# A fixed order of TensorE's instructions through an attention stage, with merge products dealt out between its steps

## The chip, the core and the metric

The kernel runs on one core of a Trainium2 chip. The metric is the device time of one execution in microseconds (us), median of several runs. The engines have queues of their own and meet through semaphores: TensorE (PE; its weight loads are shown as PEld) multiplies into PSUM, VectorE (DVE) and ScalarE (ACT) work on PSUM and SBUF, GpSimd (POOL) on SBUF alone, SyncE (SP) issues most DMAs, and ACT issues a few.

## The reference

One decoder layer on 512 tokens of width 1024, in float32. The input is normalized and projected; three mixers work on the projection (sparse attention, a spatial-gating MLP, RWKV-7); each result is gated, projected to 1024 channels and merged, and an output projection, a gated embedding and a last normalization follow.

```python
proj = h @ w_in[i]
y_nsa = _nsa(...)      # attention: block-compressed, selected and window keys
y_sg = _spatial_gating(...)
y_rk = _rwkv7(...)
ys = jnp.stack([y_nsa * jax.nn.silu(nz), y_sg * jax.nn.silu(sz), y_rk * jax.nn.silu(rz)], axis=2)
zs = jnp.einsum('bsnc,ncd->bsnd', ys, w_branch[i])
merge = jax.nn.sigmoid(mg).reshape(B, S, N_BRANCHES, D)
x = x + jnp.sum(merge * zs, axis=2) @ w_o[i]
```

Attention has 8 heads in 2 groups and works on query blocks of 128 tokens. With 512 tokens all eight selection blocks are always chosen, so the kernel computes the selected and the window part as causal attention over all keys up to the query block, and the compressed part as attention over 31 blocks.

## The kernel before

Products keep float32 precision by splitting operands into a high half (float32r) and a remainder: where both operands are split, a product is three matmuls, high x high, high x low, low x high. Weights come by DMA as `wr` (SP), ACT casts the high half `wh`, and POOL (in some stages DVE) subtracts for the low half `wl` (`wload`, L67 to L80). `fm_block` (L150) makes one block of 128 output channels for all 512 tokens: 8 x 3 matmuls of 512 columns from the normalized input (`hH`, `hL`), or 4 x 3 from a mixer's output (`ysH`, `ysL`), into a PSUM tile `mm_ps` of a pool of two.

A merge of branch b (L789) runs over m = 0 to 7: a gate block (24 matmuls, tanh by ACT into `sg`), a product block (12 matmuls), and an evacuation by DVE into `macc` (b = 1) or into `sg` and then by POOL into `macc` (b = 2, 0). Six gate blocks of b = 1 were made earlier and come back from DRAM. Branch 1 is the spatial gating, 2 the RWKV mixer, 0 attention; the first two don't need attention, the third needs all of it.

Attention (L814 to L889) goes over query blocks i = 3, 2, 1, 0 (512, 384, 256, 128 keys). For each block, eight small products give the block scores `sc_c` of all heads, and DVE and ACT make the block probabilities `pcm` from them. For each group g of four heads, `pcm` is transposed (`pc_ps`), spread by DVE (`pd`), split into `ph` and `pl`, and begins the output `o_ps` (one buffer). For b = 0, 1 (selected, window) and four heads hh there are scores `s_ps` (three buffers: two matmuls with keys `kst`, one that adds the causal mask), their maximum `mx` (DVE), the exponential with its sum (ACT), a reciprocal and a product with the gate (DVE, `sm`), and a scaling of the probabilities `P` (two heads by DVE, one by ACT, one by POOL). For each key tile kt, four transpositions give `p_ps`; ACT casts the high half `ph`, DVE subtracts for the low half `pl`, and two matmuls add to `o_ps`, the one with `pl` first. At the end of a group ACT copies half of `o_ps` (`ot`) and DVE adds both halves into `nsaY`.

A scheduler with a timing model of its own puts the instructions of each engine in order; program order is only its priority. So the merge products of branches 1 and 2, which stand behind attention in the program, go wherever it finds attention's next instruction not ready. `HOLD` (L31) keeps the last four of them until four late points of attention. Then `nsaY` is multiplied by `zs`, the gate path that is loaded from DRAM into an `sg` buffer (L898 to L901), split into `ysH` and `ysL`, and branch 0 is merged. The pool `ep` (L905: `x1`, `pp`, `fg`) is opened after attention's pools are closed, and its first loads (L910, from ACT's queue) wait until attention's tiles are let go.

Of the kernel before, what the change touches and what calls it, by code (L numbers as in the profile page):

```python
# [19 lines left out]
NG = 6  # L20
# [10 lines left out]
HOLD = (-1,) * 12 + (3, 4, 5, 6)  # L31
# [14 lines left out]
def hybrid_kernel(ctx, tc, x, p, norm_g, w_in, cmp_w1, cmp_w2, cmp_pe, sg_ln_g, sg_ln_b, sg_w, sg_b,  # L46
# [14 lines left out]
    def mm(o, a, b, start, stop, **kw):  # L61
        return PE.matmul(o, a, b, start=start, stop=stop, **kw).ins  # L62
# [726 lines left out]
    def merge(b, yH, yL, first, fin, after=()):  # L789
        for m in range(8):  # L790
          with ExitStack() as es:
            if m < len(after) and after[m] is not None:
                es.enter_context(tc.issue_after(after[m]))
            sg = gp.tile([128, 512], F32, tag="sg", name="sg")
# [12 lines left out]
            fm_block(m * 128, 128, ev_b, w_branch[b], yH, yL, 4)
# [5 lines left out]
    anch = []  # L813
    for i in ATT:  # L814
        isl = slice(i * 128, (i + 1) * 128)
        W = (i + 1) * 128
        sc = aps.tile([128, 8, 64], F32, tag="pt", name="sc_c", bufs=BP)
        for h in range(8):
            mm(sc[:, h, :], qst[:, h // 2, h % 2, isl], kcst[:, h // 4].rearrange("p a n -> p (a n)"), True, True)
# [10 lines left out]
        gv = gate[:, i, :].rearrange("p (h b) -> p b h", b=3)  # L830
# [5 lines left out]
        for g in range(2):  # L836
            o_ps = aps.tile([128, 512], F32, tag="o", name="o_ps", bufs=BO)
            pc_ps = aps.tile([128, 128], F32, tag="pt", name="pc_ps", bufs=BP)
            PE.transpose(pc_ps, pcm[:, 4 * g:4 * g + 4, :].rearrange("p h n -> p (h n)"), ident)
            pd = ap_.tile([128, 4, 128], F32, tag="pd", name="pd", bufs=1)  # L840
            ph = ap_.tile([128, 512], R, tag="ph", name="ph", bufs=3)
            pl = ap_.tile([128, 512], R, tag="pl", name="pl", bufs=3)
            V.tensor_tensor(pd, pc_ps.unsqueeze(1).to_broadcast([128, 4, 128]),
                            hm.unsqueeze(2).to_broadcast([128, 4, 128]), OP.mult)
            pd2 = pd.rearrange("p h t -> p (h t)")
            S.copy(ph, pd2)
            V.tensor_tensor(pl, pd2, f(ph), OP.subtract)
            mm(o_ps, vcst[:, g, :], ph, True, False)
            mm(o_ps[0:64], vcst[:, g, 0:64], pl, False, False)
            for b in range(2):  # L850
                P = ap_.tile([128, 4, 512], F32, tag="P", name="P")
                mx = ap_.tile([128, 4], F32, tag="mx", name="mx")
                sm = ap_.tile([128, 4], F32, tag="sm", name="sm")
                for hh in range(4):
                    h = g * 4 + hh
                    s_ps = aps.tile([128, 512], F32, tag="s", name="s_ps", bufs=BS)
                    qs = qst[:, h // 2, h % 2, isl]
                    mm(s_ps[:, :W], qs, kst[b][:, g, 0, :W], True, False)
                    mm(s_ps[:, :W], qs, kst[b][:, g, 1, :W], False, False)
                    mm(s_ps[:, i * 128:W], identb, trib, False, True)  # L860
                    V.tensor_reduce(mx[:, hh:hh + 1], s_ps[:, :W], axis=AX.X, op=OP.max, negate=True)  # L861
                    S.activation(P[:, hh, :W], s_ps[:, :W], AF.Exp, bias=mx[:, hh:hh + 1],  # L862
                                 accum_out=sm[:, hh:hh + 1])
                V.reciprocal(sm, sm)
                V.tensor_tensor(sm, sm, gv[:, 1 + b, g * 4:g * 4 + 4], OP.mult)
                for hh in range(4):
                    if PS[hh] == "S":
                        S.activation(P[:, hh, :W], P[:, hh, :W], AF.Copy, scale=sm[:, hh:hh + 1])
                    else:
                        (G if PS[hh] == "G" else V).tensor_scalar(P[:, hh, :W], P[:, hh, :W], sm[:, hh:hh + 1],  # L870
                                                                  None, op0=OP.mult)
                for kt in range(i + 1):
                    p_ps = aps.tile([128, 512], F32, tag="pt", name="p_ps", bufs=BP)
                    for hh in range(4):
                        PE.transpose(p_ps[:, hh * 128:hh * 128 + 128], P[:, hh, kt * 128:kt * 128 + 128], ident)  # L875
                    ph = ap_.tile([128, 512], R, tag="ph", name="ph", bufs=3)
                    pl = ap_.tile([128, 512], R, tag="pl", name="pl", bufs=3)
                    S.copy(ph, p_ps)  # L878
                    V.tensor_tensor(pl, p_ps, f(ph), OP.subtract)  # L879
                    mm(o_ps[0:64], vst[:, kt, b, g, 0:64], pl, False, False)  # L880
                    last = mm(o_ps, vst[:, kt, b, g, :], ph, False, b == 1 and kt == i)
            anch.append(last)
            ot = ap_.tile([64, 512], F32, tag="ot", name="ot", bufs=1)
            S.copy(ot, o_ps[64:128])
            o4 = o_ps.rearrange("p (a e t) -> p a e t", a=2, e=2)
            t4 = ot.rearrange("p (a e t) -> p a e t", a=2, e=2)
            for e in range(2):
                V.tensor_tensor(nsaY[e * 64:e * 64 + 64, 2 * g:2 * g + 2, isl], o4[0:64, :, e, :], t4[:, :, e, :],
                                OP.add)  # L889
    at_ctx.close()  # L890
    nsa_ctx.close()

    hold = [None if h < 0 else anch[h] for h in HOLD]
    merge(1, y1H, y1L, True, lambda m: None, hold[:8])
# [128 lines left out]
```

## Time and profile before

| | us |
|---|---|
| median of 3 runs (lowest to highest) | 746.05 (745.58 to 747.11) |
| the profiled execution's own time | 744.63 |
| its span, first to last instruction | 742.8 |
| TensorE busy | 714.5 (96%) |
| DVE, ACT, POOL busy | 408.6, 353.8, 287.0 |
| attention, first to last score product | 378.1 to 547.1 |

The shares are averages over stages. TensorE's busy time contains modelled ends: a matmul of 512 columns is shown 0.39 us long, while the next starts 0.23 us after it, so a wait is best read from the distance of two starts. An idle time at the end of a row names what ended it.

### The profile page before, as it was taken

What the parts mean: (1) busy time and instruction counts of PE and PEld (TensorE: products, weight loads), DVE (VectorE), ACT (ScalarE), POOL (GpSimd) and SP (SyncE); (2) the same over time, 40 slices, a digit from 0 to 9 for tenths busy, and PEclk for the clock granted to TensorE, in tenths of its full rate; (3) what the DMA queues carried; (4) which work ended last, traced back from release to release, by engine and by line L of the source; (5) the groups of instructions that cost most, each with busy time, mean ns of one, the idle gap of its engine ahead of it and who ended that gap; (6) DMA issues with size and microseconds to landing.
All of it is one profiled execution on the core that took longest, in us unless ns stands there. A gap on an engine that the chain in (4) does not pass through costs nothing.

```text
span 742.8 us, 13074 instructions
## 1 busy us (share of the span) xinstructions
PE 714.5 (96%) x4941; PEld 606.7 (82%) x4941; DVE 408.6 (55%) x776; ACT 353.8 (48%) x743; POOL 287.0 (39%) x275
## 2 busy tenths in 40 slices
PE   4999999999999999989999999989999999999995
PEld 4888788999878987779877778867877888998995
DVE  6531587758843863565676565397555223226345
ACT  6554555542363342335565554576554333227453
POOL 6444640120220263300144345333445565356563
PEclk9999999999999999999999999999999999999999
DMA  5853122125536364427433212201228334132212
GB/s 194 188 140 100 48 81 71 41 85 146 156 105 224 101 184 117 116 86 232 124 97 103 58 43 71 71 16 42 53 62 268 96 91 127 59 114 72 80 63 114
DMA packets 106689, 78.73 MB, mean 106 GB/s; under 512 B 5569, under 2 KB 97282, under 8 KB 106626
## 3 DMA queue, kind: packets, MB, share of 16 engines
q1 hardware_dynamic: 105890, 75.27, 35.5%
q10 hardware_dynamic: 736, 2.63, 0.9%
q8 instruction: 39, 0.64, 0.4%
q14 instruction: 24, 0.20, 0.1%
HBM read 67.91 MB, written 9.96 MB: 105 GB/s over the span
## 4 chain that ended last, share of the span: by engine, by line
PE 88%; DVE 4%; ACT 2%; DMA 2%; issue 1%; POOL 1%; SPq 1%; ACTq 0%; POOLq 0%; DVEq 0%
PE mm_ps L62 70%; PE s_ps L62 3%; PE o_ps L62 2%; PE g_ps L62 2%; PE p_ps L875 2%; DMA w1t<-in_cmp_w_dram 1%; PE Yp L62 1%; DVE mx L861 1%; PE u_ps L62 1%; ACT wh L78 1%; PE xt_ps L222 1%; PE r_ps L62 1%; PE mx_ps L62 1%; DVE pl L879 1%; PE bk_ps L477 1%
## 5 line engine op out<-in xcount | busy, mean ns | idle before, releaser
L79 POOL TENSOR_TENSOR wl<-wr,wh 128x512 fp32r<-128x512 f32 x144 | 192.6, 1346 | 278.9 <-ACT wh L78 257.6
L78 ACT CAST wh<-wr 128x512 fp32r<-128x512 f32 (+1 forms) x194 | 119.4, 620 | 166.5 <-PE mm_ps L62 114.9
L62 PE MATMUL mm_ps<-hH,wh 128*128 128x512 f32 (+1 forms) x440 | 174.9, 398 | 3.3 <-ACT wh L78 1.9
L62 PE MATMUL mm_ps<-hL,wh 128*128 128x512 f32 (+1 forms) x440 | 171.6, 390 | 0.0
L62 PE MATMUL mm_ps<-hH,wl 128*128 128x512 f32 (+1 forms) x440 | 171.1, 389 | 0.0
L62 PEld LDWEIGHTS mm_ps<-hH,wh 128*128 128x128 f32 x440 | 83.5, 190 | 20.7 <-ACT wh L78 2.2
L62 PEld LDWEIGHTS mm_ps<-hH,wl 128*128 128x128 f32 x440 | 83.2, 189 | 17.4 <-issue 0.2
L62 PEld LDWEIGHTS mm_ps<-hL,wh 128*128 128x128 f32 x440 | 83.6, 190 | 16.5 <-issue 0.2
L62 PE MATMUL mm_ps<-wh,hL 128*128 128x256 f32 (+1 forms) x224 | 65.0, 291 | 0.0
L62 PE MATMUL mm_ps<-wh,hH 128*128 128x256 f32 (+1 forms) x224 | 63.8, 286 | 0.0
L62 PE MATMUL mm_ps<-wl,hH 128*128 128x256 f32 (+1 forms) x224 | 63.7, 285 | 0.0
L79 DVE TENSOR_TENSOR wl<-wr,wh 128x512 fp32r<-128x512 f32 (+1 forms) x50 | 38.0, 768 | 26.8 <-ACT wh L78 26.7
L62 PEld LDWEIGHTS mm_ps<-wh,hL 128*128 128x128 f32 x224 | 42.2, 188 | 1.1 <-issue 0.5
L62 PEld LDWEIGHTS mm_ps<-wh,hH 128*128 128x128 f32 x224 | 42.1, 188 | 1.2 <-issue 0.5
L62 PEld LDWEIGHTS mm_ps<-wl,hH 128*128 128x128 f32 x224 | 42.2, 188 | 0.5
L879 DVE TENSOR_TENSOR pl<-p_ps,ph 128x512 fp32r<-128x512 f32 x40 | 27.1, 685 | 25.7 <-ACT ph L878 25.6
L62 PE MATMUL mm_ps<-ysH,wh 128*128 128x512 f32 x96 | 38.6, 402 | 0.1
L62 PE MATMUL mm_ps<-ysL,wh 128*128 128x512 f32 x96 | 38.4, 400 | 0.2 <-DVE ysL L725 0.2
L62 PE MATMUL mm_ps<-ysH,wl 128*128 128x512 f32 x96 | 38.2, 398 | 0.0
L862 ACT ACTIVATE P<-s_ps,mx 128x512 f32<-128x512 f32 (+3 forms) x64 | 33.4, 531 | 7.9 <-DVE mx L861 5.5
L62 PE MATMUL mm_ps<-wh,mH 128*128 128x256 f32 x128 | 35.9, 286 | 0.0
L62 PE MATMUL mm_ps<-wl,hT 128*128 128x256 f32 x128 | 35.8, 281 | 0.0
(337 smaller groups left out, 1434.6 us busy)
## 6 DMA issues: line engine op xcount, KB each, us to landing
wr<-in_w_in_dram SPq DMA_DIRECT2D x130, 256.0 KB
wr<-in_w_branch_dram SPq DMA_DIRECT2D x24, 256.0 KB
wr<-in_w_o_dram SPq DMA_DIRECT2D x16, 256.0 KB
wr<-in_w_ple_gate_dram SPq DMA_DIRECT2D x16, 256.0 KB
xs__129<-in_x_dram SPq DMA_DIRECT2D x4, 512.0 KB
w1t<-in_cmp_w_dram SPq DMA_DIRECT2D x4, 512.0 KB
x<-in_x_dram ACTq DMA_DIRECT2D x4, 512.0 KB
out_dram<-x SPq DMA_DIRECT2D x8, 256.0 KB
```

What stands on the lines that cost most here:

```text
L62: return PE.matmul(o, a, b, start=start, stop=stop, **kw).ins
L78: S.copy(h[:, :m], raw[:, :m])
L79: ph_["l"].tensor_tensor(l[:, :m], raw[:, :m], f(h[:, :m]), OP.subtract)
L222: PE.transpose(ps[:, k, :], xs_[:, t, (4 * a + k) * 128:(4 * a + k + 1) * 128], ident)
L477: PE.transpose(ps[:, c - c0, :], bk[:, c, 0:2].rearrange("p s t -> p (s t)"), ident)
L861: V.tensor_reduce(mx[:, hh:hh + 1], s_ps[:, :W], axis=AX.X, op=OP.max, negate=True)
L862: S.activation(P[:, hh, :W], s_ps[:, :W], AF.Exp, bias=mx[:, hh:hh + 1], accum_out=sm[:, hh:hh + 1])
L875: PE.transpose(p_ps[:, hh * 128:hh * 128 + 128], P[:, hh, kt * 128:kt * 128 + 128], ident)
L879: V.tensor_tensor(pl, p_ps, f(ph), OP.subtract)
```

## The change

TensorE's order through attention and through the merges of branches 1 and 2 is written out. The attention code is cut into acts: `cmp_` (block scores and `pcm`), `pc_` (transposition of `pcm`, P), `oc_` (first two matmuls of `o_ps`, C), `s_` (scores of one head with what follows, S0 to S3), `t_` (transposition of a key tile, T0 to T3), `o_` (its two matmuls, O0 to O3). A step is one (i, g, b), sixteen in all. In a step stand the scores S of the *next* step and the T, C, O of this one, in the order of the table `ORD`. `merge_gen` yields once ahead of every merge matmul, and `deal(n)` lets n of them go: 16 after the first scores (15 matmuls, since the first call only opens the block), 8 behind the first `pc_`, and 25 in each step, evenly spread over its acts. All of these matmuls are kept in program order (`keep_in_program_order`); the other engines are still ordered by the scheduler. A block's weights are asked for when the block ahead of it begins. `HOLD` goes. The loads of `nz` go into slices of `pp` instead of `sg` buffers.

```diff
-HOLD = (-1,) * 12 + (3, 4, 5, 6)
+FILL = (16, 8, 25)
...
+    def blk_gen(ws, srcH, srcL, nk, evac, ahead):
+
+        hs, ls = ws
+        ahead()
+        ps = pmm.tile([128, 512], F32, tag="mm", name="mm_ps")
+        for k in range(nk):
+            for j, (w, s) in enumerate(((hs, srcH), (hs, srcL), (ls, srcH))):
+                yield
+                pin(PE.matmul(ps, w[k], s[:, k, :], start=k == 0 and j == 0, stop=k == nk - 1 and j == 2))
+        evac(ps)
...
+    def o_(i, g, b, kt):
+        o_ps = ops[i, g]
+        ph, pl = trp.pop(kt)
+        mmp(o_ps[0:64], vst[:, kt, b, g, 0:64], pl, False, False)
+        mmp(o_ps, vst[:, kt, b, g, :], ph, False, b == 1 and kt == i)
...
+    ORD = {3: "S0 T0 C S1 T1 S2 O0 T2 S3 O1 T3 O2 P O3", 2: "S0 T0 C S1 T1 S2 O0 S3 T2 O1 P O2",
+           1: "S0 T0 C S1 S2 T1 S3 O0 P O1", 0: "S0 T0 C S1 S2 S3 P O0"}
+    fill = merge_gen(((1, y1H, y1L, True), (2, y2H, y2L, False)))
+
+    def deal(n):
+        for _ in range(n):
+            next(fill, None)
+
+    steps = [(i, g, b) for i in ATT for g in range(2) for b in range(2)]
+    cmp_(3)
+    for hh in range(4):
+        s_(*steps[0], hh)
+    deal(FILL[0])
+    pc_(3, 0)
+    deal(FILL[1])
+    for n, (i, g, b) in enumerate(steps):
+        nx = steps[n + 1] if n + 1 < len(steps) else None
+        acts = []
+        if (g, b) == (1, 0) and i > 0:
+            acts.append(lambda i=i: cmp_(i - 1))
...
+        tot = FILL[2]
+        for j, act in enumerate(acts):
+            act()
+            deal((j + 1) * tot // len(acts) - j * tot // len(acts))
+    for _ in fill:
+        pass
     at_ctx.close()
     nsa_ctx.close()
 
-    hold = [None if h < 0 else anch[h] for h in HOLD]
-    merge(1, y1H, y1L, True, lambda m: None, hold[:8])
-    merge(2, y2H, y2L, False, lambda m: None, hold[8:])
     y0H, y0L = ytiles()
-    for q in range(4):
-        zs = gp.tile([128, 512], F32, tag="sg", name="zs")
...
+    for q in range(4):
+        zs = pp[:, q, 0:512]
+        SY.dma_start(zs, dr["nz"][q * 128:(q + 1) * 128, :])
+        V.tensor_tensor(nsaY[:, q, :], nsaY[:, q, :], zs, OP.mult)
+        split(y0H[:, q, :], y0L[:, q, :], nsaY[:, q, :], 0.5)
```

The first place is TensorE at the beginning of attention, around the first `pc_ps`. Before:

```order
L62 MATMUL mm_ps<-ysH,wh 128x512
L62 MATMUL mm_ps<-ysL,wh 128x512
L62 MATMUL mm_ps<-ysH,wl 128x512
L62 MATMUL mm_ps<-ysH,wh 128x512
L62 MATMUL mm_ps<-ysL,wh 128x512
L839 MATMUL pc_ps<-ident,pcm 128x128
L875 MATMUL p_ps<-ident,P 128x128 x4
L62 MATMUL s_ps<-kst_3737,qst 128x512 x2
```

It stood behind all four score groups of the second step (`kst_3738`) and the merge products around them. On the same engine at the same place, now:

```order
L858 MATMUL s_ps<-trib,identb 128x128
L799 MATMUL mm_ps<-ysH,wh 128x512
L799 MATMUL mm_ps<-ysL,wh 128x512
L799 MATMUL mm_ps<-ysH,wl 128x512
L799 MATMUL mm_ps<-ysH,wh 128x512
L799 MATMUL mm_ps<-ysL,wh 128x512
L799 MATMUL mm_ps<-ysH,wl 128x512
```

The first of these rows ends the fourth score group of the first step; nine more products of the same kind follow, and then:

```order
L799 MATMUL mm_ps<-ysH,wl 128x512
L887 MATMUL pc_ps<-ident,pcm 128x128
L799 MATMUL mm_ps<-ysH,wh 128x512
L799 MATMUL mm_ps<-ysL,wh 128x512
L799 MATMUL mm_ps<-ysH,wl 128x512
L799 MATMUL mm_ps<-ysH,wh 128x512
L799 MATMUL mm_ps<-ysL,wh 128x512
```

So `pc_ps` now comes 15 products behind the first step's scores and ahead of the second step's. DVE's order between the block scores and the last step of `pcm` is nearly the same as before, 21 instructions now and 23 before.

The second place is TensorE at the end of the first step (block i = 3), from the transposition T3 on:

```order
L930 MATMUL p_ps<-ident,P 128x128 x4
L799 MATMUL mm_ps<-ysH,wh 128x512
L799 MATMUL mm_ps<-ysL,wh 128x512
L858 MATMUL o_ps<-pl,vst 64x512
L858 MATMUL o_ps<-ph,vst 128x512
L799 MATMUL mm_ps<-ysH,wl 128x512
L799 MATMUL mm_ps<-ysH,wh 128x512
L858 MATMUL o_ps<-pl,vst 64x512
L858 MATMUL o_ps<-ph,vst 128x512
L799 MATMUL mm_ps<-ysL,wh 128x512
L799 MATMUL mm_ps<-ysH,wl 128x512
L858 MATMUL s_ps<-kst_3737,qst 128x512 x2
```

Before, six or more merge and score products stood between a transposition and the two matmuls that use it; now T3 and O3 are two pairs of products and O2 apart.

The third place is ACT behind the last group of attention (`ot`), before:

```order
L884 COPY ot<-o_ps 64x512
L910 DMA x_6129<-in_x_dram 128x1024 x2
L724 ACTIVATE ysH<-nsaY 128x512
L910 DMA x_6129<-in_x_dram 128x1024
L724 ACTIVATE ysH<-nsaY 128x512
L910 DMA x_6129<-in_x_dram 128x1024
```

Two of the four splits into `ysH` and the casts of the next weights stood ahead of this row. The same place now:

```order
L942 COPY ot<-o_ps 64x512
L1005 DMA x_6109<-in_x_dram 128x1024
L824 ACTIVATE sg<-mm_ps 128x512
L1005 DMA x_6109<-in_x_dram 128x1024 x3
L724 ACTIVATE ysH<-nsaY 128x512
L1006 DMA fg<-in_final_norm_g_dram 128x1024
L78 CAST wh<-wr 128x512 x2
L724 ACTIVATE ysH<-nsaY 128x512
L78 CAST wh<-wr 128x512
L724 ACTIVATE ysH<-nsaY 128x512
```

All four splits now stand behind the copy, and the casts of the weights of branch 0's first gate block (the row of two) behind the first split. TensorE has 22 matmuls of branch 2 behind the last value products, and then that gate block. In SP's queue the four `nz` loads stand in one row, with the following weight loads behind them.

## Rows read from the trace of the kernel before

**Rows 1.** Page, part 1: busy us (share of span) x instructions, whole span
```profile
PE 714.5 (96%) x4941; PEld 606.7 (82%) x4941; DVE 408.6 (55%) x776; ACT 353.8 (48%) x743; POOL 287.0 (39%) x275
```

**Rows 2.** Windows: busy us (x) of PE, PEld, DVE, ACT, POOL; PEclk; DMA; GB/s
```profile
480.00:566.00 86.00, 80.87 (x438) 63.93 (x436) 61.05 (x147) 50.56 (x138) 34.01 (x29) 0.98 0.21 56
542.00:549.00 7.00, 5.46 (x26) 4.17 (x26) 6.01 (x16) 4.77 (x15) 3.56 (x3) 0.76 0.16 47
```

**Rows 3.** Waits of PE, 480 to 566: us, times, longest
```profile
PE o_ps L62 <- DVE pl L847: 2.1, 2, 1.2
```

**Rows 4.** Timeline of PE, 542 to 549: start, duration, line, what, idle before
```profile
542.64 0.48 PE L62 MATMUL o_ps<-ph,vcst 128*128 128x512 f32 x1
544.30 0.44 PE L62 MATMUL o_ps<-pl,vcst 128*64 128x512 f32 x1 [1.18 <-DVE pl L847]
...
548.75 0.39 PE L62 MATMUL mm_ps<-hH,wl 128*128 128x512 f32 x1
548.98 0.39 PE L62 MATMUL mm_ps<-hH,wh 128*128 128x512 f32 x1
```

**Rows 5.** Timeline of DVE, first and last step of the first block softmax
```profile
378.54 0.42 DVE L823 TENSOR_TENSOR pcm<-sc_c,cmask 128x256 f32<-128x256 f32 x1
...
389.95 0.92 DVE L835 TENSOR_TENSOR pcm<-pcm,sm 128x256 f32<-128x256 f32 x1
```

**Rows 6.** Timeline of PE, the same stretch
```profile
378.06 0.19 PE L62 MATMUL sc_c<-kcst,qst 128*128 128x64 f32 x1
...
393.97 0.27 PE L839 MATMUL pc_ps<-ident,pcm 128*128 128x128 f32 x1
394.08 0.60 PE L875 MATMUL p_ps<-ident,P 128*128 128x128 f32 x4
394.43 0.71 PE L62 MATMUL s_ps<-kst,qst 128*128 128x512 f32 x2
...
395.03 0.71 PE L62 MATMUL s_ps<-kst,qst 128*128 128x512 f32 x2
```

**Rows 7.** Groups of DVE by form, 376 to 566: busy us, mean ns, idle before
```profile
L879 DVE TENSOR_TENSOR pl<-p_ps,ph 128x512 fp32r<-128x512 f32 x40 | 27.1, 685 | 25.7 <-ACT ph L878 25.6
L861 DVE TENSOR_REDUCE mx<-s_ps 128x1 f32<-128x512 f32 x16 | 10.8, 682 | 3.3 <-PE s_ps L62 3.2
L861 DVE TENSOR_REDUCE mx<-s_ps 128x1 f32<-128x384 f32 x16 | 8.5, 548 | 0.5 <-PE s_ps L62 0.4
...
L865 DVE TENSOR_TENSOR sm<-sm,gate 128x4 f32<-128x4 f32 x16 | 4.9, 308 | 0.2
L870 DVE TENSOR_SCALAR P<-P,sm 128x512 f32<-128x512 f32 x8 | 4.8, 642 | 0.1
...
L870 DVE TENSOR_SCALAR P<-P,sm 128x384 f32<-128x384 f32 x8 | 4.2, 567 | 0.1
```

**Rows 8.** Groups of ACT by form, 376 to 566
```profile
L78 ACT CAST wh<-wr 128x512 fp32r<-128x512 f32 x38 | 23.5, 620 | 22.6 <-PE mm_ps L62 17.1 <-POOL wl L79 2.3 <-issue 2.1
...
L862 ACT ACTIVATION_READ_ACCUMULATOR P<-s_ps,mx 128x1 f32 x64 | 13.0, 204 | 0.0
L862 ACT ACTIVATE P<-s_ps,mx 128x512 f32<-128x512 f32 x16 | 10.9, 690 | 3.9 <-DVE mx L861 3.7
L862 ACT ACTIVATE P<-s_ps,mx 128x384 f32<-128x384 f32 x16 | 9.2, 586 | 0.2
```

**Rows 9.** Timeline of all engines, end of attention, 553 to 572
```profile
553.48 0.50 SPq L899 DMA_DIRECT2D zs<-dr_nz  x1
...
556.65 0.69 DVE L900 TENSOR_TENSOR nsaY<-nsaY,zs 128x512 f32<-128x512 f32 x1 [1.78 <-DMA zs<-dr_nz]
...
558.68 1.30 POOL L79 TENSOR_TENSOR wl<-wr,wh 128x512 fp32r<-128x512 f32 x1 [2.44 <-ACT wh L78]
...
562.39 0.40 PE L62 MATMUL o_ps<-ph,vst 128*128 128x512 f32 x1
...
564.60 0.85 ACTq L910 DMA_DIRECT2D x<-in_x_dram  x2
```

More of the change, by code (lines that the diff above doesn't have):

```diff
@@ L787, in hybrid_kernel, with merge_gen, ask, ev_b @@
     macc = gp.tile([128, 8, 512], F32, name="macc", bufs=1)
[L789 to L794, printed above, removed]
+    pin = tc.keep_in_program_order
+    def blk_gen(ws, srcH, srcL, nk, evac, ahead):
[7 more added lines that the diff above has]
+        evac(ps)
+    def merge_gen(jobs):
+        todo = []
+        for b, yH, yL, first in jobs:
+            for m in range(8):
+                if not (b == 1 and m < NG):
+                    todo.append((b, m, "g", yH, yL, first))
+                todo.append((b, m, "o", yH, yL, first))
+        got = {}
+        def ask(n):
+            if n < len(todo) and n not in got:
+                b, m, kind, *_ = todo[n]
+                got[n] = (wparts([(w_in, O_MG + b * 1024 + m * 128, 128)], 8) if kind == "g"
+                          else wparts([(w_branch[b], m * 128, 128)], 4))
+        ask(0)
+        sg = None
+        for n, (b, m, kind, yH, yL, first) in enumerate(todo):
+            if kind == "g" or (b == 1 and m < NG):
+                sg = gp.tile([128, 512], F32, tag="sg", name="sg")
+            if kind == "g":
+                yield from blk_gen(got.pop(n), hH, hL, 8,
+                                   lambda ps, sg=sg: S.activation(sg, ps, AF.Tanh, scale=0.5), lambda: ask(n + 1))
+                continue
             if b == 1 and m < NG:
                 SY.dma_start(sg, dr["sg"][m * 128:(m + 1) * 128, :])
-            else:
-                fm_block(O_MG + b * 1024 + m * 128, 128, lambda ps: S.activation(sg, ps, AF.Tanh, scale=0.5))
-            def ev_b(ps):
+            def ev_b(ps, m=m, sg=sg, first=first):
                 if first:
@@ L804, in ev_b, with merge @@
                     V.scalar_tensor_tensor(sg, sg, 1.0, ps, op0=OP.add, op1=OP.mult)
-                    (V if b == 0 and m == 7 else G).tensor_tensor(macc[:, m, :], macc[:, m, :], sg, OP.add)
+                    G.tensor_tensor(macc[:, m, :], macc[:, m, :], sg, OP.add)
+            yield from blk_gen(got.pop(n), yH, yL, 4, ev_b, lambda: ask(n + 1))
+    def merge(b, yH, yL, first, fin):
+        for m in range(8):
+            sg = gp.tile([128, 512], F32, tag="sg", name="sg")
+            fm_block(O_MG + b * 1024 + m * 128, 128, lambda ps: S.activation(sg, ps, AF.Tanh, scale=0.5))
+            def ev_b(ps):
+                V.scalar_tensor_tensor(sg, sg, 1.0, ps, op0=OP.add, op1=OP.mult)
+                (V if m == 7 else G).tensor_tensor(macc[:, m, :], macc[:, m, :], sg, OP.add)
                 fin(m)
@@ L835, in hybrid_kernel @@
         V.tensor_tensor(pcm, pcm, sm8.unsqueeze(2).to_broadcast([128, 8, 32]), OP.mult)
[L836 to L882, printed above, removed]
@@ new lines, in cmp_, with hilo, pc_ @@
+        pcms[i] = pcm
+    def hilo():
+        return (ap_.tile([128, 512], R, tag="ph", name="ph", bufs=3), ap_.tile([128, 512], R, tag="pl", name="pl", bufs=3))
+    def pc_(i, g):
+        pc_ps = aps.tile([128, 128], F32, tag="pt", name="pc_ps", bufs=BP)
+        pin(PE.transpose(pc_ps, pcms[i][:, 4 * g:4 * g + 4, :].rearrange("p h n -> p (h n)"), ident))
+        pd = ap_.tile([128, 4, 128], F32, tag="pd", name="pd", bufs=1)
+        V.tensor_tensor(pd, pc_ps.unsqueeze(1).to_broadcast([128, 4, 128]),
+                        hm.unsqueeze(2).to_broadcast([128, 4, 128]), OP.mult)
+        pd2 = pd.rearrange("p h t -> p (h t)")
+        ph, pl = pcs[i, g] = hilo()
+        S.copy(ph, pd2)
+        V.tensor_tensor(pl, pd2, f(ph), OP.subtract)
```

67 lines of the change are left out of this document (57 added, 10 removed).

## The prediction

> **What bounds the kernel now.** I read the page's head first: TensorE is busy for 96% of the span [rows 1], so only its waits and its clock can give time back. Then the windows: from 376 to 480 us it never shows idle; from 480 to 566 us, the attention's second half, it is busy for 80.87 of 86 us [rows 2]. The list of waits puts the largest share of the 5.13 us on DVE's low halves of the attention weights [rows 3]. Last, TensorE's own rows: products of 512 columns start 0.23 us apart, but each is shown 0.39 long, so an idle hides about 0.17 more [rows 4]. Nine such waits hide 1.5 us; waits under 0.17, which no row shows as idle, I estimate at 1 us more. So the attention loses about 7.5 us (5.1 to 8.5). Behind the worst wait, before the row at 544.30, the granted clock falls to the lower of its two levels, 1.2 GHz instead of 2.4; over 542 to 549 us it averages 0.76 [rows 2, 4], which costs 7 x 0.24 = 1.7 us. Together 9.2 us could go.
>
> The profile's own execution took 744.63 us (span 742.8); the median of the timed runs is 746.05, 1.4 more. I work from 744.63 and add 1.4 at the end.
>
> **The change part by part.** The number of products, casts, reductions and loads stays. What goes is the freedom in TensorE's order: before, a scheduler placed ready merge products wherever attention was late, and from 376 to 480 us that covered everything. Now about 25 products a step are dealt out, two or three between one act and the next, and an act whose input is late holds all products behind it. So I take the whole 9.2 us off and then ask at each act whether its input is there.
>
> The Trainium skill, "TensorE: Matmul & The Clock Gate", section "Step-by-step: what each phase is for", says that only weight loads are pulled ahead, while "the MATMULs themselves stay in program order". The row at 544.30 [rows 4] agrees: TensorE stood 1.18 us although products that need nothing from attention followed. Could ready products pass a late one, the start and the steps below would cost nothing; by the rule they cost in full.
>
> *The start.* The first transposition of the block probabilities, pc_ps, now stands behind eight small score products, four score groups and only 15 merge products. Before, it came 15.9 us after the last small score product (378.06 to 393.97 [rows 6]). TensorE's work ahead of it now: 0.9 us for the eight (an estimate, under the 8 x 0.19 shown), 4 x 0.60 for the groups (394.43 to 395.03 [rows 6]), 15 x 0.23; in all 6.8 us. DVE must work through 21 instructions in its own order until pcm is ready: block softmax, four maxima, both halves of a key evacuation, one merge evacuation, two scalings. Before, the same work took from 378.54 to 390.87, 12.3 us, nearly without a gap, with two others in between, a maximum and a merge evacuation, some 0.6 each [rows 5, 7]; so 11.1 now. The first of them starts 0.48 us behind the last small product (378.06 to 378.54 [rows 5, 6]), so pcm is ready at 0.8 + 0.48 + 11.1 = 12.4 us. TensorE waits 5.6 us: part of it at the fourth score group, whose PSUM buffer is freed by the first exponential, and at the second merge block, whose buffer hangs on DVE's key evacuation, the rest at pc_ps. Bounds 3.5 (DVE 2 us quicker) to 6.5. I take 5.5.
>
> *The steps.* With 512 columns (block i=3) a step ends S3 O1 T3 O2 O3, two products behind each. From the end of S3, O3 is due after O1 (two products of 0.23), T3 (0.4, from 394.08 to 394.43 [rows 6] and a slower start behind it), O2 and eight products: 0.46 + 0.4 + 0.46 + 8 x 0.23 = 3.2 us. But DVE takes the low half of T3 only behind the scalings that follow S3's exponential: maximum 0.68, exponential 0.69, read-out of its sum 0.20, product with the gate 0.31, two scalings of 0.64, low half 0.69 [rows 7, 8]: 3.85 us, and the reciprocal and four handovers some 0.35 more: 4.2. O3 is 1.0 us late. Where a transposition of block probabilities with two more products stands before O3, it is due 0.6 later: 0.4 late. For the other group one product fewer stands there: 1.2 late. In block i=2 (384 columns) the low half of T2 hangs on S3 in the same way: 0.55 + 0.59 + 0.20 + 0.31 + 2 x 0.57 + 0.69 + 0.35 = 3.8 us [rows 7, 8] against about 2.5 us of TensorE work (S3, T2, O1, O2), or 3.1 with the extra transposition: 1.3 and 0.7 late. With 256 and 128 columns the maxima and scalings are shorter and the transposition is not the last but one act: nothing, or some tenths. Four steps of 512 or so (1.0, 0.4, 1.2, 0) and four of 384 (1.3, 0.7, 1.3, 0.4) give 6.6; one late act gives the next a little slack, so I take 6.0. Bounds 0, if DVE and ACT run ahead, to 9, if the single o_ps buffer is late as well.
>
> *The tail.* The four nz loads go into pp, part of a pool that lies where attention's tiles lay. Before, they went into sg buffers, the first at 553.48, during attention [rows 9]. Now SP can issue them only when attention has let go, and the weight loads of the next blocks wait behind them in SP's queue; ACT's casts of the next merge block's weights stand behind the first split, which needs the first load. From the last value product: 564.60 - 562.39 = 2.2 us until such a release (the x loads' issue shows it), 3.17 from a nz load's issue to its use (553.48 to 556.65), product with it 0.69, split 0.62 (taken as a cast), cast 0.62: 7.3 us; the POOL half of the weights 1.30 more: 8.6 [rows 8, 9]. TensorE has one value product and 22 others left, 5.3 us. The third block starts 2.0 late and its third product 0.8 later still; a merge addition on POOL ahead of the weights' low half, likewise held by DVE, adds some tenths: 3.2. Bounds 1.5 to 6.
>
> The Trainium skill, "DMA: Bandwidth & Descriptors", section "Issuing engines are not separate DMA queues", says that loads of ACT and SP run on the same engines and interleave. ACT's x loads, 512 KB each, are let go by the same release, so by the rule the first nz load shares with one: I estimate 1.2 us more, a tail of 4.4. No run shows these two together; the sum stays at 3.2, the bound of 6 has it.
>
> *The clock.* 1.43 us lost before 544.30 (1.66 between starts, for 0.23 [rows 4]) and more right behind brought the lower level for a stretch that cost 1.7. The start loses 5.5 us within some 9, the tail 3.2 within 4. Each can bring such a stretch; part of the first falls into the wait. I take 2.5 (0 to 5).
>
> Sum: 744.63 - 9.2 + 5.5 + 6.0 + 3.2 + 2.5 = 752.6; on the scale of the medians 754.0.
>
> **Rivals.** (a) *Faster.* The chain from S3 to the last value product is hidden: handovers are short, DVE and ACT are ahead by more than I reckon, the weights of the third block are cast before the tail's wait. Then only the start is left: 744.63 - 9.2 + 5.5 + 1.4 = 742.3. It decides at the last value product of a 512-column step: due 3.2 us behind S3; if its input takes less, this is right. For it: DVE is busy for only 61 of the 86 us from 480 on [rows 2], and the products are spread evenly. Against it: the sum of durations alone is 3.85.
> (b) *No change.* Start and tail as above, steps and clock at nothing or a single clock stretch: 744.63 - 9.2 + 5.5 + 3.2 + 1.4 = 745.5, up to 747.2. For it: in the second half of attention DVE has slack, which may absorb the small step waits.
> (c) *Much slower: weights late.* POOL makes the low halves of the merge weights in order, and its probability scaling, which waits for DVE's sums, stands among them. If each of the eight wide steps holds a low half (1.30 [rows 9]) until TensorE stands, 8 x 1.3 = 10.4 come on top: 764. Against it: POOL is the idlest of the engines [rows 1] and weights are asked for one block ahead.
> (d) The change doesn't do what it says: the written order comes out as before. The two orders differ at every place quoted above; little chance.
>
> **How the numbers follow.** About 0.2% (1.5 us) is what a measurement of this kernel can tell from no change. Forecast (749 to 760) 0.60, (a) 0.10, (b) 0.15, (c) 0.12, (d) 0.03. (b) and (d) split between same and slower by a little: faster 0.12, same 0.13, slower 0.75. The range must reach from (b) to the near side of (c): 745 to 761; the forecast alone would be 749 to 760.
>
> **What would show it.** In the profile after: TensorE waiting for pc_ps on DVE's pcm, once, for over 2 us, early in attention; a wait of about 1 us before the last value product's low-half operand in each wide step but the fourth; a wait for ACT's weight cast some 5 us behind the last value product, with ysH before it and a nz load before that; the granted clock below 1 behind the first and the last. No wait for pcm, and this forecast is wrong by its largest term; waits for wl on POOL would speak for (c).

## The result, and the profile after

The changed kernel takes 759.61 us (753.86 to 760.76, 6 runs), the kernel before 746.28 (745.58 to 747.11, 6 runs): a ratio of 1.0168, interval 1.0135 to 1.02. It is slower by 13.3 us; the prediction said 754.0, 8.0 more than before. The profiled execution took 760.74. The page, as [rows 1]:

```profile
span 759.0 us, 13075 instructions
PE 722.1 (95%) x4941; PEld 609.7 (80%) x4941; DVE 415.2 (55%) x776; ACT 355.9 (47%) x743; POOL 288.2 (38%) x275
```

The same 4941 matmuls, but the span is 16.2 us longer. The windows, as [rows 2], show where TensorE stands now (busy time of PE, PEld, DVE, ACT, POOL, then the clock):

```profile
376.00:396.00 20.00, 16.12 (x71) 11.94 (x70) 14.15 (x27) 11.60 (x24) 7.08 (x5) 0.96 0.30 79
396.00:480.00 84.00, 79.80 (x415) 59.37 (x414) 57.45 (x110) 47.85 (x107) 28.73 (x21) 0.99 0.20 53
480.00:566.00 86.00, 83.49 (x444) 67.64 (x443) 49.31 (x117) 48.55 (x128) 39.65 (x34) 0.98 0.21 57
566.00:590.00 24.00, 21.41 (x82) 16.04 (x81) 11.87 (x12) 7.60 (x14) 10.28 (x8) 0.93 0.62 216
```

Two rows of the kernel before, for stretches that [rows 2] leaves out:

```profile
376.00:480.00 104.00, 104.00 (x516) 81.29 (x515) 61.70 (x114) 57.17 (x124) 46.13 (x34) 1.00 0.27 74
566.00:590.00 24.00, 23.63 (x102) 18.94 (x102) 7.04 (x8) 9.35 (x17) 15.39 (x12) 1.00 0.62 205
```

Before, TensorE was fully busy from 376 to 480 us, lost 5.1 us from 480 to 566, and 0.4 from 566 to 590. Now the second half of attention loses 2.5, but the start 3.9, the steps up to 480 us 4.2, the tail 2.6. The list of waits from 370 to 600 us, as [rows 3], names them; these are the six largest of eight:

```profile
PE o_ps L858 <- DVE pl L933: 5.9, 6, 2.1
PE pc_ps L887 <- DVE pcm L879: 2.5, 1, 2.5
PE mm_ps L62 <- ACT ysH L724: 1.6, 1, 1.6
PE mm_ps L62 <- DVE ysL L725: 0.9, 2, 0.7
PE mm_ps L799 <- DVE kst L763: 0.8, 1, 0.8
PE s_ps L858 <- ACT P L915: 0.6, 1, 0.6
```

The start, as [rows 5, 6]: TensorE's rows that waited, and DVE's last rows ahead of `pcm`.

```profile
385.13 0.73 PE L858 MATMUL s_ps<-kst,qst 128*128 128x512 f32 x2 [0.57 <-ACT P L915]
...
389.62 0.51 PE L799 MATMUL mm_ps<-ysH,wh 128*128 128x512 f32 x1 [0.84 <-DVE kst L763]
...
393.05 0.33 PE L887 MATMUL pc_ps<-ident,pcm 128*128 128x128 f32 x1 [2.46 <-DVE pcm L879]
```

```profile
391.14 1.32 DVE L923 TENSOR_SCALAR P<-P,sm 128x512 f32<-128x512 f32 x2
392.38 0.16 DVE L878 TENSOR_TENSOR sm<-sm,gate 128x8 f32<-128x8 f32 x1
392.57 0.42 DVE L879 TENSOR_TENSOR pcm<-pcm,sm 128x256 f32<-128x256 f32 x1
```

DVE's chain, from 382.79 to 392.99, took 10.2 us; the three waits are the three that were named. A step, the third of block i=3: DVE, then TensorE.

```profile
433.72 0.18 DVE L917 RECIPROCAL sm<-sm 128x4 f32<-128x4 f32 x1 [0.92 <-ACT P L915]
433.93 0.17 DVE L918 TENSOR_TENSOR sm<-sm,gate 128x4 f32<-128x4 f32 x1
434.13 1.32 DVE L923 TENSOR_SCALAR P<-P,sm 128x512 f32<-128x512 f32 x2
435.37 0.68 DVE L933 TENSOR_TENSOR pl<-p_ps,ph 128x512 fp32r<-128x512 f32 x1
```

```profile
434.32 0.40 PE L799 MATMUL mm_ps<-hH,wl 128*128 128x512 f32 x1
436.10 0.45 PE L858 MATMUL o_ps<-pl,vst 128*64 128x512 f32 x1 [1.39 <-DVE pl L933]
```

The low half `pl` for O3 stands behind two scalings of the next step's P, and O3 starts 1.78 us behind its predecessor instead of 0.23.

To add up the waits that no row shows as idle, I took for every matmul of both traces the distance to the next start, less the usual distance between two such shapes. Waits, and what the lower clock added, in us:

| | before | after |
|---|---|---|
| start (376 to 396) | 0.2 | 4.6 |
| steps (396 to 566) | 6.8 | 8.9 |
| tail (566 to 592) | 0.6 | 3.7 |
| lower clock, 376 to 592 | 1.5 | 4.7 |
| sum | 9.0 | 21.9 |

The rest of the span's 16.2 us lies ahead of attention, where TensorE's order is the same in both kernels: the same matmul starts at 324.93 before and at 329.37 after, 4.4 us late, and 3.7 of these came as the clock fell at 217 us (1.5) and at 323 us (2.2) in this execution. The window behind the first fall, before and then after:

```profile
218.00:222.00 4.00, 4.00 (x39) 3.05 (x39) 1.81 (x3) 2.15 (x4) 0.00 (x0) 1.00 0.92 238
218.00:222.00 4.00, 4.00 (x13) 3.20 (x14) 1.85 (x4) 2.15 (x4) 0.01 (x1) 0.72 0.77 220
```

**bef2** below tells whose doing the second is. So 11.8 us arise from attention on; the table says 12.9, and some 1 us is the error of its method.

### The profile page after: what moved, and what is told of

The parts are those of the page before. It is cut to its first block, busy times and chain, and to the rows that moved or that the text cites. A ratio compares the mean times of both kernels' runs of the same rounds, so it can differ in the third digit from the quotient of the medians.

```text
span 759.0 us, 13075 instructions
## 1 busy us (share of the span) xinstructions
PE 722.1 (95%) x4941; PEld 609.7 (80%) x4941; DVE 415.2 (55%) x776; ACT 355.9 (47%) x743; POOL 288.2 (38%) x275
## 4 chain that ended last, share of the span: by engine, by line
PE 82%; DVE 9%; ACT 3%; DMA 3%; issue 2%; POOL 1%; SPq 1%; POOLq 0%; ACTq 0%; DVEq 0%
PE mm_ps L62 55%; PE mm_ps L799 10%; PE s_ps L858 3%; PE o_ps L858 2%; PE g_ps L62 2%; PE p_ps L930 2%; DMA w1t<-in_cmp_w_dram 1%; DVE P L923 1%; DVE mx L914 1%; PE Yp L62 1%; DVE pl L933 1%; DMA pp<-dr_nz 1%; ACT P L915 1%; PE r_ps L62 1%; PE u_ps L62 1%
## 5 line engine op out<-in xcount | busy, mean ns | idle before, releaser
L62 PE MATMUL mm_ps<-hH,wh 128*128 128x512 f32 (+1 forms) x360 | 143.1, 397 | 3.7 <-ACT wh L78 2.1
L62 PE MATMUL mm_ps<-hL,wh 128*128 128x512 f32 (+1 forms) x360 | 140.5, 390 | 0.0
L62 PE MATMUL mm_ps<-hH,wl 128*128 128x512 f32 (+1 forms) x360 | 140.5, 391 | 0.0
L62 PEld LDWEIGHTS mm_ps<-hH,wh 128*128 128x128 f32 x360 | 69.1, 192 | 18.4 <-ACT wh L78 2.4
L62 PEld LDWEIGHTS mm_ps<-hH,wl 128*128 128x128 f32 x360 | 68.8, 191 | 14.7 <-issue 0.2
L62 PEld LDWEIGHTS mm_ps<-hL,wh 128*128 128x128 f32 x360 | 68.9, 191 | 14.1 <-issue 0.2
L914 DVE TENSOR_REDUCE mx<-s_ps 128x1 f32<-128x512 f32 (+3 forms) x64 | 30.9, 487 | 26.8 <-PE s_ps L858 26.6
L62 PE MATMUL mm_ps<-wh,lT 128*128 128x256 f32 x128 | 35.8, 281 | 0.0
L62 PE MATMUL mm_ps<-wl,mH 128*128 128x256 f32 x128 | 35.7, 281 | 0.0
```

## The experiments

Each is timed against the kernel before on the same chip; the chips differ between some of the experiments, so the ratios compare better than the times: one hundredth of a ratio is 7.5 us. Where a sum of waits is given, it is made as in the table, from waits over 0.15 us; the changed kernel's steps have 8.2 so counted.

**ctl**, nothing edited.

> The changed kernel once more, nothing edited. In its first profile 3.7 us were lost to the lower clock level at 217 and 322 to 329 us, in a part whose TensorE work and order are those of the kernel before. Theory: whether such a stretch falls there is settled anew in each execution and has nothing to do with the change. Then the median is 759 to 760, some executions come out near 754, the profile may lack one or both stretches, and the kernel before shows such executions too, 3 to 5 us above its others. Rival: the change brings them about. Then nearly all executions of this kernel have them (clock 0.980 to 0.984) and none of the kernel before.

758.73 us (753.39 to 761.21), ratio 1.0159 (1.0132 to 1.0185); before 746.56 (745.0 to 747.26). All waits of the first profile are there to within some hundredths; the clock falls at 321 us but not at 217. No execution of before was above 747.3, which spoke for the rival; **bef2** decides for the fall near 320 us.

**tail**, the nz loads in sg buffers again:

```diff
-        zs = pp[:, q, 0:512]
+        zs = gp.tile([128, 512], F32, tag="sg", name="zs")
```

> Undoes the tail part alone: the nz loads go into sg buffers again. Theory: the waits at 577 to 581 us (0.9 + 1.8 + 0.5 us) and the lower clock behind them (1.6 us) go, about what the kernel before had there (0.56) stays: 4.2 to 4.8 us less than the changed kernel, about 755. Rival: the loads then wait for the two sg buffers, which the merge in the attention holds to its end, and the first split comes as late: no change, 759 to 760.

759.62 us, ratio 1.0182 (1.0164 to 1.02): no change. One wait of 3.7 us replaces those of 0.9 and 1.8 (waits counted as in the table). So the new place of these loads is not by itself what costs, and the rival held.

**start**, the second key block (`evk[1]` is its evacuation) behind the eight small products:

```diff
+    evk = {}
...
-        fm_block((O_NKS, O_NKW)[b], 128, ev_k)
+        evk[b] = ev_k
+    fm_block(O_NKS, 128, evk[0])
...
     cmp_(3)
+    for _ in blk_gen(wparts([(w_in, O_NKW, 128)], 8), hH, hL, 8, evk[1], lambda: None):
+        pass
```

> Takes away the start's wait alone: the second key block (24 products, 5.6 us) moves behind the eight small score products, so that TensorE has 12.4 us of work between them and the first transposition of the block probabilities, and DVE's chain needs about 12. Theory: the waits at 384 to 393 us (4.6 us) go and the lower clock behind them (1.6) too: 5 to 6 us less than the changed kernel, about 754. Rival: the scores' exponentials are now late instead, and the first transposition of P waits for them: 1 to 3 us less.

753.72 us, ratio 1.0096 (1.008 to 1.0113): 5.0 us under ctl. The wait for `pcm` is gone, a wait of 1.0 us for the fourth score group's buffer and one of 0.5 are left, so 4.6 us of waits became 1.6, and the clock does not fall at the start. The theory held in the main; the late exponential of the rival is the wait of 1.0. In this profile the clock does not fall at 487 us either, though the wait ahead of it is as it was, so not all of the 5.0 need be the start's.

**steps**, the last value product behind the next step's first score group:

```diff
+    late = None
...
+        if late:
+            acts.insert(1, late)
+            late = None
+        if i >= 2:
+            late = acts.pop()
```

> Takes away the waits in the steps alone: in the blocks i=3 and i=2 the last value product of a step is put behind the first score group of the next one, some 1.2 us of TensorE work later. Theory: of the waits at 408, 421, 434, 447, 459, 471 and 483 us (1.1, 0.3, 1.6, 0.2, 1.1, 0.5, 2.3 us, 7.2 in all) about 5.5 to 6.5 go, and the lower clock at 487 us (1.6) with them: 7 to 8 us less than the changed kernel, about 752. Rival: DVE is the bound in these steps and the waits move to the next transposition or value product: 0 to 3 us less.

756.98 us, ratio 1.0144 (1.0124 to 1.0163): 1.8 us under ctl. The waits in the steps fall from 8.2 to 6.0; they moved to the single `o_ps` buffer, whose evacuation is now late (0.9 and 1.2 us), and to other value products. The rival was nearer.

**ord**, the last transposition ahead of the last score group, in i=3 and in the same way in i=2:

```diff
-    ORD = {3: "S0 T0 C S1 T1 S2 O0 T2 S3 O1 T3 O2 P O3", 2: "S0 T0 C S1 T1 S2 O0 S3 T2 O1 P O2",
+    ORD = {3: "S0 T0 C S1 T1 S2 O0 T2 O1 T3 S3 O2 P O3", 2: "S0 T0 C S1 T1 S2 O0 T2 S3 O1 P O2",
```

> Only the written order of the wide steps is changed: the last transposition of a step stands before its last score group instead of behind it (i=3: O1 T3 S3 O2 P O3; i=2: O0 T2 S3 O1 P O2). In the changed kernel's profile DVE makes the low half that O3 waits for at 433.51 us, behind the two scalings of the next step's P (432.27, 1.32 us), for which nothing is in a hurry; putting O3 later (the run before) moved the waits and took only 2 to 3 us off. Theory: it is DVE's order; with the low half ahead of the scalings 6 to 7 of the 7.2 us in the steps go, and the lower clock at 487 us (1.6): about 751. Rival: the total of DVE's work in a step is the bound, and the next step's first transposition now waits for the scalings: 0 to 3 us less, 756 or more.

759.34 us, ratio 1.0175 (1.0162 to 1.0188): nothing gained. The waits for `pl` are gone from the list, and these stand there:

```profile
PE o_ps L858 <- DVE nsaY L946: 2.6, 3, 1.5
...
PE p_ps L930 <- DVE P L923: 2.4, 7, 0.4
```

The next step's first transposition now waits for the scaled P, and the block product C for the evacuated `o_ps`. The steps have 8.6 us of waits, against 8.2: the rival held.

**dveq**, DVE's order instead of TensorE's: the reciprocal, and with it all scalings (`m_`, cut out of `s_`), behind the last low half.

```diff
+    def m_(i, g, b, held):
...
+        r_ = V.reciprocal(sm, sm)
+        if held:
+            pin(r_)
...
+                    t_(i, g, b, int(w[1]))
+                    if i >= 2 and int(w[1]) == i:
+                        m_(*nx, True)
```

> TensorE's order is that of the changed kernel; only DVE's is edited: in blocks i=3 and i=2 the reciprocal, the product with the gate and the scalings of the next step's P stand behind the low half of the step's last transposition, not ahead of it. Moving the value product or the transposition in TensorE's order moved the waits without ending them. Theory: the wait is for DVE's order inside the step, not for its amount of work. The low half is ready about 3.1 us behind S3 (product and transposition ahead of it 1.8, cast 0.6, itself 0.7) and due at 3.2; P is scaled by 4.4 and due at 5.0: of the 7.2 us at least 5 go, and the lower clock behind 483 us: 752 to 754. Rival: DVE's work in a wide step is the bound, and the first transposition of the next step then waits for P as it did with the transposition moved: 2 us or less, 757 or more.

756.82 us, ratio 1.0134 (1.0116 to 1.0152). The seven waits for `pl` in the wide steps fall from 7.2 us to 1.5, as the theory had it, but 3.4 us of waits for P came in their place, so the time is the rival's. TensorE's rows of the largest of these waits, and POOL's rows at the same time:

```profile
433.84 0.44 PE L935 MATMUL p_ps<-ident,P 128*128 128x128 f32 x2 [0.28 <-DVE P L928]
435.27 0.33 PE L935 MATMUL p_ps<-ident,P 128*128 128x128 f32 x1 [0.99 <-POOL P L928]
```

```profile
432.07 1.43 POOL L79 TENSOR_TENSOR wl<-wr,wh 128x512 fp32r<-128x512 f32 x1 [4.22 <-ACT wh L78]
433.48 1.73 POOL L928 TENSOR_SCALAR P<-P,sm 128x512 f32<-128x512 f32 x1
```

The reciprocal held back POOL's and ACT's scalings too, and POOL took a weight's low half first. I had moved more than the two instructions that stood in the way.

**xlate**, the x and fg loads behind the last split of y0 (`sp`) on ACT:

```diff
+        sp = split(y0H[:, q, :], y0L[:, q, :], nsaY[:, q, :], 0.5).ins
+    with tc.issue_after(sp):
+        for t in range(4):
+            S.dma_start(x1[:, t, :], x[t * 128:(t + 1) * 128, :])
+        S.dma_start(fg, final_norm_g.unsqueeze(0).to_broadcast([128, 1024]))
```

> The four x loads and the load of fg (512 KB each, ACT's queue), which start as attention ends, are put behind the last split of y0 on ACT; the nz loads stay in pp. Theory: these loads slow the nz loads and the next weights (DMA 99% and 400 GB/s from 565 to 576 us; the nz products start at 569.6, 572.1, 576.2, 579.3 us). Without them the four splits come 3.5 to 7 us earlier: of the waits in the tail (0.9 + 1.8 + 0.5) at least 2 go and the lower clock behind them (1.5) perhaps: 2 to 4.5 us less than the changed kernel, 755 to 757. Rival: the release at attention's end alone is what counts (the first split needs 7 us from there, my reckoning before the run): under 1 us less.

753.97 us (750.71 to 757.06), ratio 1.0106 (1.0083 to 1.0129): 4.8 to 5.6 us under the changed kernel (4.0 to 4.6 by the ratios, as **ctl** ran on another chip). The waits in the tail fall from 3.2 to 0.8 us, and the clock does not fall behind them. Nor does it in this profile at the start and at 487 us, where the waits are as they were; so some of the gain may be chance, but 2.4 us are the tail's waits. The rival is refuted. The rows, first of the changed kernel, answering to [rows 9]: SP's issue, DVE's products with nz and splits, and the POOL work and the largest TensorE wait of the same time:

```profile
567.25 1.76 SPq L1001 DMA_DIRECT2D pp<-dr_nz  x4
...
571.44 0.69 DVE L1002 TENSOR_TENSOR nsaY<-nsaY,pp 128x512 f32<-128x512 f32 x1 [4.26 <-DMA pp<-dr_nz]
573.82 0.84 DVE L1002 TENSOR_TENSOR nsaY<-nsaY,pp 128x512 f32<-128x512 f32 x1 [1.08 <-DMA pp<-dr_nz]
574.58 3.48 DVE L725 SCALAR_TENSOR_TENSOR ysL<-nsaY,ysH 128x512 fp32r<-128x512 f32 x2
577.98 1.79 DVE L1002 TENSOR_TENSOR nsaY<-nsaY,pp 128x512 f32<-128x512 f32 x1
...
574.07 5.16 POOL L79 TENSOR_TENSOR wl<-wr,wh 128x512 fp32r<-128x512 f32 x3
...
580.49 0.50 PE L62 MATMUL mm_ps<-ysH,wh 128*128 128x512 f32 x1 [1.64 <-ACT ysH L724]
```

and of xlate:

```profile
563.57 1.76 SPq L1002 DMA_DIRECT2D pp<-dr_nz  x4
...
566.72 0.69 DVE L1003 TENSOR_TENSOR nsaY<-nsaY,pp 128x512 f32<-128x512 f32 x1 [3.22 <-DMA pp<-dr_nz]
567.87 0.69 DVE L1003 TENSOR_TENSOR nsaY<-nsaY,pp 128x512 f32<-128x512 f32 x1 [0.47 <-DMA pp<-dr_nz]
```

From the issue to the first use it takes 4.19 us beside the x loads and 3.15 without; to the second 6.57 and 4.30. The third product of the changed kernel, at 577.98, shows no idle ahead of it: DVE was still at the two splits, which with it took 5.2 us beside POOL's three low halves, where one of each takes 0.69 undisturbed. So the wait at 580.49 comes from late loads and from a slowed DVE together; no run separates the two.

**all**, the edits of start, ord and xlate together.

> Three edits together: the second key block behind the eight small products, the last transposition before the last score group, the x loads behind the splits. Theory: the three places are independent and their gains add: 759.2 - 5.5 - 7.5 - 3 = 743, 3 us less than the kernel before. Rival: TensorE's freedom before was worth more than these waits, and what is gained in one place is lost in the next: 748 or more.

751.98 us, ratio 1.0069 (1.0057 to 1.0082). Start and tail gain as each did alone; the steps keep 8.6 us of waits, as in ord. The rival's number held.

**all2**, the same with dveq's edit for that of ord.

> The same order on DVE, with the second key block behind the eight small products and the x loads behind the splits of y0, TensorE's order in the steps as in the changed kernel. Theory: the gains at the three places add: 759.2 - 5.5 (start) - 5.2 (tail) - 5 to 6.5 (steps) = 742 to 743.5, below the kernel before. Rival: as with the three edits before, the steps keep their waits: 749 to 751.

748.99 us, ratio 1.0028 (1.0015 to 1.0041). The steps keep 6.9 us of waits. That is the rival, at the lower edge of its 749 to 751.

**bef2**, the kernel before, profiled a second time.

> The kernel before once more, for a second profile. Its executions fall into two groups, 745.0 to 745.8 (clock 0.991 to 0.994) and 746.6 to 747.3 (0.986 to 0.989). Theory: the difference is a lower-clock stretch at 217 or at 318 to 327 us, as in the changed kernel's profiles; this profile then shows one, with 746.6 or more, or shows none with 745.8 or less. Rival: these stretches belong to the changed kernel alone, and a profile with 746.6 or more has its lower clock elsewhere.

747.03 us (745.0 to 747.5), ratio 1.0009 (1.0 to 1.0019); the profiled execution took 745.0. Windows of the kernel before, first profile (744.63 us), and then of this one:

```profile
318.00:322.00 4.00, 2.04 (x45) 1.66 (x44) 3.97 (x9) 0.85 (x3) 0.00 (x0) 1.00 0.43 133
322.00:326.00 4.00, 3.48 (x42) 2.82 (x39) 2.43 (x8) 1.59 (x3) 0.00 (x0) 1.00 0.03 11
```

```profile
318.00:322.00 4.00, 2.33 (x34) 2.04 (x36) 3.89 (x8) 0.77 (x2) 0.00 (x0) 0.77 0.43 133
322.00:326.00 4.00, 3.48 (x40) 3.08 (x39) 2.04 (x6) 0.60 (x2) 0.00 (x0) 0.50 0.00 0
326.00:330.00 4.00, 4.00 (x17) 3.23 (x16) 1.33 (x4) 1.64 (x3) 1.64 (x1) 0.88 0.17 66
```

The same instructions and waits, once at 2.4 GHz and once some 7 us at 1.2: the lower clock at 320 us is not the change's doing. The fall at 217 us stands in neither profile of the kernel before and in five of the twelve of the changed kernel and its variants, so whose doing it is stays open. But this profile has no fall at 545 us, so my sorting was wrong: an execution of 745.0 has one such stretch too. Those of 746.6 and more may have both; no profile shows one.

**free**, the merge products no longer held in order:

```diff
-                pin(PE.matmul(ps, w[k], s[:, k, :], start=k == 0 and j == 0, stop=k == nk - 1 and j == 2))
+                PE.matmul(ps, w[k], s[:, k, :], start=k == 0 and j == 0, stop=k == nk - 1 and j == 2)
```

> The changed kernel with one thing undone: the merge products are no longer held in the written order, so the scheduler places them again where it expects attention to be late; the attention's own acts, the loads and the tail stay as changed. Theory: the fixed order is what costs at the start (4.6 us of waits, 1.6 of lower clock) and in the steps (8.2 and 1.6), the tail has other causes and stays: some 8 to 11 us less than the changed kernel, 748 to 751. Rival: the calculated chain from scores to scaled P is too long for any order of these products, and as many waits come back in other places: 755 or more.

752.9 us, ratio 1.0083 (1.0067 to 1.0098), less gain than expected. Its windows and waits:

```profile
396.00:480.00 84.00, 84.00 (x433) 66.37 (x433) 49.74 (x97) 47.42 (x105) 35.57 (x27) 1.00 0.24 63
480.00:555.00 75.00, 75.00 (x422) 62.45 (x420) 49.26 (x115) 42.81 (x117) 36.76 (x31) 1.00 0.23 61
555.00:575.00 20.00, 9.71 (x34) 6.33 (x33) 9.47 (x22) 7.28 (x18) 1.88 (x2) 0.66 0.52 190
```

```profile
PE mm_ps L62 <- ACT ysH L724: 6.9, 1, 6.9
PE o_ps L858 <- ACT P L915: 2.0, 1, 2.0
PE o_ps L858 <- DVE pl L933: 1.4, 1, 1.4
PE mm_ps L799 <- DVE kst L763: 1.1, 1, 1.1
```

From 396 to 555 us TensorE never shows idle. But the products are used up by then, and the end of attention and the tail stand bare: 10.3 us of waits (the first three of the list), and a clock of 0.66 over 20 us. Both theory and rival missed this.

**all3**, the edits of start and xlate, and three for what all2 left, in place of dveq's: only DVE's two scalings stand behind the last low half (`pl_`), six products ahead of the fourth score group at the start, C one act later.

```diff
...
+            if behind is not None:
+                es.enter_context(tc.issue_after(behind))
...
+                    pl_ = t_(i, g, b, int(w[1]))
+                    if i >= 2 and int(w[1]) == i:
+                        m_(*nx, pl_)
...
+        if hh == 3:
+            deal(6)
...
+    ORD = {3: "S0 T0 S1 C T1 S2 O0 T2 S3 O1 T3 O2 P O3", 2: "S0 T0 S1 C T1 S2 O0 S3 T2 O1 P O2",
+           1: "S0 T0 S1 C S2 T1 S3 O0 P O1", 0: "S0 T0 S1 C S2 S3 P O0"}
```

> The second key block behind the eight small products, the x loads behind the splits of y0, and three edits for the waits that were left there: at the start six merge products ahead of the fourth score group (its buffer was 1.0 us late); in the steps only DVE's two scalings stand behind the last low half, the reciprocal, the gate product and the scalings on ACT and POOL no longer (POOL's was 1.0 us late, ACT's 0.7); the block products C stand one score group later (0.3 to 0.8 us late each time). Theory: each of these waits is a queue's order; 4 to 6 of the 9 us left in the attention go: 743 to 745 against 749 without these edits, below the kernel before. Rival: the waits move on again, as twice before: 747 to 749.

742.46 us (741.24 to 744.01), ratio 0.9946 (0.9928 to 0.9963): 4.4 us under the kernel before, 16 to 17 under the changed one. Its waits, 370 to 600 us:

```profile
PE o_ps L861 <- DVE pl L945: 1.2, 2, 1.0
PE mm_ps L802 <- DVE kst L765: 0.8, 1, 0.8
PE mm_ps L62 <- DVE ysL L725: 0.8, 2, 0.7
```

The steps are down to 2.2 us, and no clock falls from 376 to 592 us, though it does at 217 and 323. The theory held. The three new edits were run together only, so what each of them gives is not known.

## Why the prediction was right, and where its terms were off

It was slower, within the range, by the mechanism forecast: an act whose input is late holds everything behind it. The number was 5.6 us too low, and 759.61 lies at the far end of the 749 to 760 that I gave the forecast alone. Two terms were too small, the steps and the clock, and one was of the right size for a wrong reason, the tail. The terms, against the tables above:

- *Taken off, 9.2.* The table of before has 9.0, and nearly all of it went. Of the 3.1 us of waits that the changed kernel has in the second half of attention, 2.3 are one of the seven at a last value product that I placed; 0.5 is at a C, where the kernel before waited longest.
- *Start, 5.5: measured 4.6.* The wait for `pc_ps` on `pcm` came, split over the three places that were named. DVE's chain took 10.2 us, not 11.1, which is the difference. **start** shows the cause: with 5.6 us of TensorE's work moved behind the small products, the wait for `pcm` went and the time fell by 5.0.
- *Steps, 6.0: measured 8.2.* For O3 in i=3 I had 1.0, 0.4, 1.2, 0 and the trace has 1.1, 0.3, 1.6, 0.2; for O2 in i=2 I had 1.3, 0.7, 1.3, 0.4 and it has 1.1, 0.5, 2.3, 0. Their sum is 7.2. My eight estimates add up to 6.3, not to the 6.6 that I wrote, and taking 6.0, because "one late act gives the next a little slack", was wrong. Most of what the seven lack is the wait at 485 us, 2.3 where I had 1.3. Two waits at C, 0.5 us each, I had not asked for. Shown: the wait is for queue order, not amount of work (**free** and **all3** do the same work nearly without it). Each of the three edits of one queue (**steps**, **ord**, **dveq**) handed much of the lateness to the next act. That no edit of one queue could do it is not shown: **dveq** moved too much, and DVE's two scalings, which **all3** moves, were not run without its later C.
- *Tail, 3.2: measured 3.2 in its three waits, 3.7 in all.* The size was right by luck, for the cause was half wrong. I charged it to the late release and to ACT's weight cast, and left the x loads to a bound. **tail** undid the place of the loads and nothing changed; **xlate** moved the x loads and the tail fell to 0.8 us. TensorE waited for the split operands themselves, not for a weight cast; the gate block that I had late came on time. That DVE's splits take 1.74 us each beside POOL's low halves, and not 0.69, and so hold up the later ones, I had not reckoned with at all. The rule of the Trainium skill, "DMA: Bandwidth & Descriptors", section "Issuing engines are not separate DMA queues", was the better guide: by it I estimated 1.2 us for the first load. The trace agrees: the runs show 4.19 - 3.15 = 1.04, and 6.57 - 4.30 = 2.27 for the second.
- *Clock, 2.5: measured 4.7 in the stretch.* This term was the most undersized for its size: the start, the steps and the tail each brought a fall of some 1.6 us; I had counted two, one of them partly inside a wait. The kernel before pays 1.5, so the net is 3.2; I had 2.5 - 1.7 = 0.8. In **start** the wait at the start went and the fall behind it too, but in **xlate** the wait stayed and the clock did not fall there. The wait of 2.3 us at the last value product near 485 us stands unchanged in five profiles, and the clock falls behind it in three of them (the changed kernel, **ctl**, **tail**) and not in **start** and **xlate**. So a wait makes a fall possible and not certain, and a term for it has to be a chance.

With the measured terms the forecast of 8.0 over before becomes 8.0 + 2.9 (steps, 8.9 with the small waits of the table, which I had taken off in the 9.2 and not put back) + 2.4 (net of the clock) - 0.9 (start) + 0.5 (tail) = 12.9, the difference of the table's sums. The two profiles differ by 11.8 from attention on, the medians by 13.3, and by 12.2 in **ctl**. Whether the clock falls more often ahead of attention in the changed kernel's executions stays open.

The rivals: (a) was refuted by the seven waits, (b) by their sum, (d) by the order that the trace shows. (c), weights late on POOL, does not appear: no `wl` is among TensorE's waits. A POOL queue that mixes low halves with scalings did cost 1.0 us once, but the other way round, in **dveq**: P was late behind a `wl`.

## What to carry to other kernels

A fixed order of the busiest engine is only as good as the order of the engines that feed it: put each producer's urgent work ahead of what is due later. Look at the whole chain before an edit, since here three edits of one queue let the wait move on, and only the run that set DVE's order and TensorE's together came below the kernel before. Spread independent work to the very end: in **free** it was used up early, and the tail stood bare. Keep large loads that nobody needs yet out of a tight stage, as **xlate** did. A wait is priced with the chance of a fall of the clock behind it.

## What the runs showed of the hardware that was not expected

- The clock on equal code: waits of 1.9 and 0.5 us near 318 us were followed by some 7 us at 1.2 GHz in the second profile of before and in all of the other kernels, and by none in the first profile of before. This stretch costs about 2 us; in the changed kernel's first profile it and the shorter one at 217 cost 3.7. Executions of one kernel differ along with the clock: in **ctl** the one of 753.4 us has a mean granted clock of 0.990, the one of 761.2 us 0.980.
- DVE and POOL slow each other in the tail: while POOL made three low halves (574.07, 5.16 us, 1.72 each against 1.30 [rows 9]), DVE's two low halves of the split took 3.48, 1.74 each, where one alone takes 0.69. The Trainium skill, "GPSIMD Engine Reference", section "1. Specifications", names this for DVE instructions with two SBUF inputs; the trace agrees. It need not be both: a DVE product with nz at 581.08 took 1.80 beside a POOL low half (581.02) that took its 1.30.
